# Per-head sums of squares by small fp32 matmuls with the squares as stationary operand, in an encoder block on one core

## The chip, the cores and the metric

The kernel runs on one core of a Trainium2 chip. The metric is the device time of one execution, in microseconds. Three runs of the kernel before gave 759.06, 760.45 and 761.18 us; the median is 760.45 us. One more execution was taken with the hardware profiler, and all times of single instructions come from it.

## The reference

One encoder layer on a sequence of 512 tokens of width 1024, all in fp32. What matters here is the attention group: the queries and the keys of eight heads are made from two small latents, and each head's 96 query numbers and 96 key numbers are normalised by their own root mean square (the key's 32 rotary numbers are shared by all heads).

```python
h = _rmsnorm(x, norm_mix)
proj = h @ w_in
c_q, c_kv, k_pe, u_h = ...                       # 768, 256, 32 and 3 * 512 wide
q  = (_rmsnorm(c_q, q_norm) @ w_uq).reshape(B, S, 8, 96)
kv = (_rmsnorm(c_kv, kv_norm) @ w_ukv).reshape(B, S, 8, 128)
k_nope, v = kv[..., :64], kv[..., 64:]
k = concatenate([k_nope, broadcast(k_pe)], -1)
q = _rmsnorm(q, qk_norm_q); k = _rmsnorm(k, qk_norm_k)
...                                              # rotary part, softmax(q k^T / sqrt(96)) v
u_h = _dwconv3(u_h); x0, x1, vh = split(u_h)     # Hyena: filters by a small sine network
y_hyena = x0 * _bidir_long_conv(x1 * vh, h_fwd, h_bwd, hyena_bias)
x = x + concatenate([_rmsnorm(y_attn), _rmsnorm(y_hyena)]) @ w_out
...                                              # gated MLP with a convolution, then an embedding term
```

## The kernel before, in words

All activations lie with the channel on the partitions and the 512 tokens along the free axis. A product of a weight with activations is done in three fp32r matmuls of 128x512: both operands are split into a high part (fp32r) and the rest, a low part, and high by high, high by low and low by high are summed in PSUM (`prod3`, `mms`, L176). The split of an activation is one ScalarE copy and one VectorE subtraction (`split`, L131 and L132, with a gain L134 and L135). Four PSUM banks named mm and four named ax are handed round.

Weights come in the order of the list `stream`. `wload` loads 128x1024 (or 128x768) by SyncE's queue, makes the high part on ScalarE (L142), and the low part in two ways: the first `cut` columns on VectorE (L143); the other columns by a negated copy on ScalarE (L145) to which a transfer on GpSimd's queue adds the weight from HBM once more (L146). There are three buffers of the high and of the low part, so the ScalarE instruction that makes the high part of a weight waits until TensorE has finished the product that used the weight three places earlier.

The order on TensorE is the order of the program text, with side work put in by a small planner: `advance(cost)` moves a clock while products are issued, and generators that are due on that clock issue their next piece between two groups of matmuls. The other engines' orders come from a scheduler with priorities (`pri`); each engine works its list strictly in that order. The stages up to the attention are:

- Input projection: 21 weights, 24 matmuls each. Two of them give the key/value latent, the third the rotary key. Beside it run two generators: `latent_kv`, which squares the two latent tiles (L519, L522), adds them into the tile accy (L523), after `D_LR` clock units makes the sum over the partitions by one fp32 matmul with a tile of ones (L220, in `rms_bcast`), and then the inverse root and the split (L205 to L216, L528, L134, L135); and `filter_task`, the sine network of the Hyena filter (three matmuls L370, each of which waits for ScalarE's sine L377 of the layer before), then the filter's transforms. `D_FT` is its start. Its last transform feeds a chain of VectorE products (L589 to L610) with eight results that ScalarE and VectorE split (L131, L132).
- UK: four products of 6 matmuls give the keys. Each is squared by `square` (L655, L131, L132) and copied (L723).
- UQ: six products of 18 matmuls give the queries, squared in the same way and copied (L773, L776). Into these the planner puts `key_task`, which sums the key squares of each head, makes 1/rms, and scales the keys; `query_scale` (turning of a row L231, four small fp32 matmuls L677); and `headsum_task`, which sums the query squares.
- The sums: `headsum` has 8 columns of 0 and 1 (`sel`) as stationary operand and the high and the low part of the squares as moving operand, two matmuls of 128x512, into 8 rows of one PSUM bank. After the last one, `rows` copies 8x512 out of PSUM on ScalarE (L667), and `turn_rows` turns it by four small transposes on TensorE (L231), so that tokens lie on the partitions; `rms_cols` does Ln, variance, Exp and one correction step on tiles of 128x32 (L205, L206, L210, L214 to L216). For the keys the result `ks` is turned back (L699), split (L701, L702) and spread over the partitions by matmuls L706.
- Then the values, the inverse transforms, and the attention (scores, softmax, transposes L942, weighing).

After the attention follow the output projection, the MLP and the embedding, which the change leaves alone.

## Time and profile before

| | before |
|---|---|
| median of 3 runs | 760.45 us |
| the profiled execution | 758.43 us |
| its span from first to last instruction | 756.6 us |
| TensorE busy | 722.1 us, 95% of the span |
| VectorE busy | 504.8 us, 67% |
| ScalarE busy | 372.2 us, 49% |
| mean granted TensorE clock | 0.991 |

1.83 us of the profiled execution lie outside the span. In a row of the timeline the first number is the start, the second the length, then engine, line, operation, output and inputs by name, and in brackets the idle time just before the row with the instruction that ended it. A row with "x6" is six instructions run together. The modelled length of a matmul overlaps the next one, so that the cost of a matmul is read from start to start.

### The profile page before, as it was taken

Reading aid. Unit: us, or ns where it says so; the run is one execution under the profiler, and the core shown is the slowest. Engines: PE = TensorE matmul, PEld = TensorE weight load, DVE = VectorE, ACT = ScalarE, POOL = GpSimd, SP = SyncE. Lnnn points to the kernel's source line nnn. Section 1 sums busy time; section 2 is a strip of 40 time slices with the busy share of each in tenths; the row PEclk is TensorE's granted clock in tenths of the full one; section 3 lists DMA queues with packets and bytes.
Section 4 is the critical chain, followed back from the end, with each engine's and each line's share of the span. In section 5 each row is a group of like instructions: output and inputs, shape, how many; then the busy total and the mean of one; then the engine's idle time right before and its main releaser. Section 6 shows DMA issues by size and latency. Waiting matters only on the chain.

```text
span 756.6 us, 9036 instructions
## 1 busy us (share of the span) xinstructions
PE 722.1 (95%) x3256; PEld 583.0 (77%) x3256; DVE 504.8 (67%) x780; ACT 372.2 (49%) x574; POOL 151.8 (20%) x150
## 2 busy tenths in 40 slices
PE   5989999996997899999999999999999999999997
PEld 4757888874675777787888888888888888888886
DVE  6479997989779987885766566666665332233382
ACT  7445455367658896463534443544353222126340
POOL 2101100111126662130422222222122000005000
PEclk9989999999899999999999999999999999999999
DMA  8844753444536210533232323232323233333331
GB/s 277 244 129 117 191 158 84 108 97 93 126 92 170 75 21 23 126 99 110 83 113 84 105 91 112 83 98 98 99 96 86 88 106 104 97 89 128 111 112 56
DMA packets 30110, 82.83 MB, mean 109 GB/s; under 512 B 3913, under 2 KB 5257, under 8 KB 30066
## 3 DMA queue, kind: packets, MB, share of 16 engines
q1 hardware_dynamic: 24418, 71.62, 31.1%
q0 software_dynamic: 5392, 10.25, 7.0%
q8 instruction: 25, 0.41, 0.2%
q10 hardware_dynamic: 256, 0.39, 0.2%
q14 instruction: 19, 0.16, 0.1%
HBM read 77.00 MB, written 2.10 MB: 105 GB/s over the span
## 4 chain that ended last, share of the span: by engine, by line
PE 54%; DVE 0%; ACT 0%; DVEq 0%; issue 0%
PE mm L176 37%; PE ax L176 17%; PE ax L220 0%; DVE t L1128 0%; ACT t L1127 0%; DVEq L1295 0%; DVE t L1129 0%
## 5 line engine op out<-in xcount | busy, mean ns | idle before, releaser
L176 PE MATMUL mm<-a,wh 128*128 128x512 f32 (+1 forms) x912 | 283.2, 392 | 8.2 <-ACT wh L273 6.5
L176 PEld LDWEIGHTS mm<-a,wh 128*128 128x128 f32 x912 | 171.0, 190 | 49.7 <-ACT wh L273 6.5
L143 DVE TENSOR_TENSOR wl<-wr,wh 128x1024 fp32r<-128x1024 f32 (+3 forms) x113 | 124.3, 1101 | 115.5 <-ACT wh L142 113.6
L142 ACT ACTIVATE wh<-wr 128x1024 fp32r<-128x1024 f32 (+1 forms) x113 | 116.5, 1031 | 162.3 <-PE mm L176 127.4
L176 PE MATMUL mm<-a,wl 128*128 128x512 f32 (+1 forms) x456 | 176.8, 388 | 0.0
L176 PE MATMUL ax<-a,wh 128*128 128x512 f32 x400 | 123.2, 389 | 0.0
L176 PEld LDWEIGHTS mm<-a,wl 128*128 128x128 f32 x456 | 86.2, 189 | 17.4 <-DVE wl L274 0.2
L176 PEld LDWEIGHTS ax<-a,wh 128*128 128x128 f32 x400 | 75.1, 188 | 15.5
L176 PE MATMUL ax<-a,wl 128*128 128x512 f32 x200 | 77.8, 389 | 0.0
L176 PE MATMUL mm<-g,wh 128*128 128x512 f32 x232 | 73.9, 401 | 1.7 <-ACT t L647 1.7
L1064 POOL TENSOR_TENSOR f<-f 128x512 f32<-128x512 f32 x22 | 28.7, 1304 | 169.2 <-DVE f L543 149.5
L176 PE MATMUL mm<-h,wh 128*128 128x512 f32 x192 | 59.0, 389 | 0.0
L176 PEld LDWEIGHTS mm<-g,wh 128*128 128x128 f32 x232 | 44.2, 192 | 12.9 <-ACT t L647 2.1
L176 PE MATMUL mm<-g,wl 128*128 128x512 f32 x116 | 46.0, 396 | 0.0
L176 PEld LDWEIGHTS ax<-a,wl 128*128 128x128 f32 x200 | 37.5, 188 | 7.9
L176 PEld LDWEIGHTS mm<-h,wh 128*128 128x128 f32 x192 | 36.0, 188 | 7.5
L1060 DVE TENSOR_TENSOR f<-mm,R 128x512 f32<-128x512 f32 x22 | 15.2, 691 | 33.7 <-PE mm L176 33.7
L176 PE MATMUL mm<-h,wl 128*128 128x512 f32 x96 | 37.3, 389 | 0.0
L536 ACT ACTIVATE f<-f,par 128x512 f32<-128x512 f32 x44 | 35.5, 808 | 1.0 <-DVE f L1060 1.0
L1063 ACT ACTIVATE f<-f 128x512 f32<-128x512 f32 x22 | 13.9, 632 | 44.5 <-DVE f L543 44.5
L146 POOL DMA_DIRECT2D wl<-in_w_in_dram x16 | 13.9, 868 | 106.0 <-ACT wl L145 53.0
L543 DVE SCALAR_TENSOR_TENSOR f<-f,par 128x511 f32<-128x511 f32 x44 | 33.8, 771 | 1.4
(312 smaller groups left out, 1015.9 us busy)
## 6 DMA issues: line engine op xcount, KB each, us to landing
wr<-in_w_up_dram SPq DMA_DIRECT2D x44, 512.0 KB, 3.5
wr<-in_w_in_dram SPq DMA_DIRECT2D x19, 512.0 KB, 3.9
wr<-in_w_down_dram SPq DMA_DIRECT2D x16, 512.0 KB, 3.5
x<-in_xT_dram SPq DMA_DIRECT2D x16, 256.0 KB, 4.3
wl<-in_w_in_dram POOLq DMA_DIRECT2D x16, 256.0 KB, 5.3
wr<-in_w_out_dram SPq DMA_DIRECT2D x8, 512.0 KB, 4.2
wr<-in_w_gate_dram SPq DMA_DIRECT2D x8, 512.0 KB, 3.5
wr<-in_w_down_dram SPq DMA_DIRECT2D x8, 384.0 KB, 3.0
```

Of the source, the lines that this page charges most:

```text
L142: S.activation(hi[:, :n], raw[:, :n], AF.Copy)
L143: V.tensor_tensor(lo[:, :cut], raw[:, :cut], f32(hi[:, :cut]), op=ALU.subtract)
L146: G.dma_start(lo[:, cut:n], src[:, cut:n], accum_op=ALU.add)
L176: last = PE.matmul(out, l, r, start=start and i == 0, stop=stop and i == n - 1)
L536: S.activation(c, z, AF.Identity, scale=pcol(w, 3 * m + 1), bias=pcol(b, m))
L543: V.scalar_tensor_tensor(c[:, 0 : T - 1], z[:, 1:T], pcol(w, 3 * m + 2), c[:, 0 : T - 1], op0=ALU.mult, op1=ALU.add)
L1060: V.tensor_tensor(z, ps_up.pop(m), R2, op=ALU.mult)
L1063: S.activation(cc[0], cc[0], AF.Silu)
L1064: G.tensor_tensor(cc[1], cc[0], cc[1], op=ALU.mult)
```

## The change

- `square` is one ScalarE instruction into a tile of its own; the split into high and low (one ScalarE copy, one VectorE subtraction) is gone, and with it the shared tile accy in between. There are ten such tiles, four for the keys and six for the queries.
- `headsum` issues four fp32 matmuls in place of two fp32r ones. 128 tokens of the squares are the stationary operand (128x128), 8 columns of `sel` the moving one; the result has tokens on the partitions and 8 columns. `rows` and the `turn_rows` of the keys' and queries' sums are gone. The keys' shared rotary square (`pesq`) goes the same way, in four small matmuls in place of one of 8x512.
- `key_task` spaces its sums by 0.9 in place of 0.5 clock units, and no longer waits `D_RC` before `rms_cols`.
- `sel` is fp32, loaded by SyncE's queue in place of GpSimd's.
- The first `cut` columns of a weight's low part, on VectorE, are 256 in place of 512 for the input projection from the sixth weight on and for the two UK/UV weights, and 256 in place of 384 for UQ. The other 768 or 512 columns take the way over ScalarE and the transfer.
- `D_LR` goes from 7 to 10 and `D_FT` from 8.5 to 11.5.

```diff
-D_LR = 7.0
+D_LR = 10.0
...
-D_FT = 8.5
+D_FT = 11.5
...
-    stream = [(w_in[m], 1024, 1024 if m < 5 else 512) for m in range(21)]
-    stream += [(w_ukn, 1024, 512)] + [(w_uq[m], 768, 384) for m in UQ] + [(w_ukv, 1024, 512)]
+    stream = [(w_in[m], 1024, 1024 if m < 5 else 256) for m in range(21)]
+    stream += [(w_ukn, 1024, 256)] + [(w_uq[m], 768, 256) for m in UQ] + [(w_ukv, 1024, 256)]
...
-    sel = const.tile([P, 56], F32R, tag="sel", name="sel")
+    sel = const.tile([P, 56], F32, tag="sel", name="sel")
...
+    SP.dma_start(sel, c_sel)
...
-        G.dma_start(sel, c_sel)
...
     def square(src):
         with pri("sq"):
-            S.activation(accy, src, AF.Square)
-            h, l = tmp(F32R), tmp(F32R)
-            split(h, l, accy)
-        return h, l
-
-    def headsum(ps, j, sq, start=False, stop=False):
-        w = sel[:, j * 8 : (j + 1) * 8]
-        mms(ps[0:8, :], [(w, sq[0]), (w, sq[1])], start=start, stop=stop)
-
-    def rows(ps):
-        r = tmp()[0:8, :]
-        with pri("rows"):
-            S.activation(r, ps[0:8, :], AF.Copy)
-        return r
+            sq = tmp()
+            S.activation(sq, src, AF.Square)
+        return sq
+
+
+    def headsum(ps, sq, w, start=False, stop=False):
+        for t in range(4):
+            PE.matmul(
+                ps[:, t * 8 : (t + 1) * 8], sq[:, t * P : (t + 1) * P], w,
+                start=start and t == 0, stop=stop and t == 3,
+            )
...
     def key_task(sqs):
         for j in range(4):
-            headsum(ssk, j, sqs[j], start=j == 0, stop=False)
-            yield 0.5
-        PE.matmul(ssk[0:8, :], ones[0:32, 0:8], pesq[0:32, :], start=False, stop=True)
-        k = rows(ssk)
-        yield D_RC
+            headsum(ssk, sqs[j], sel_of(j), start=j == 0, stop=False)
+            yield 0.9
+        headsum(ssk, pesq[0:32, :], ones[0:32, 0:8], stop=True)
         r = col("ks")
-        rms_cols(r, turn_rows(k), 96)
+        rms_cols(r, ssk[:, 0:32], 96)
         yield D_KC
...
     def headsum_task(j, sq):
-        headsum(ssq_ps, j, sq, not summed, len(summed) == 5)
+        headsum(ssq_ps, sq, sel_of(j), not summed, len(summed) == 5)
         summed.append(j)
-        if len(summed) == 6:
-            ssq_rows.append(rows(ssq_ps))
         yield None
...
-        rms_cols(v, turn_rows(ssq_rows[0]), 96, qs)
+        rms_cols(v, ssq_ps[:, 0:32], 96, qs)
```

In the changed kernel's own numbering `square` is L656, `headsum` L662, the turning of `ks` L696, its split L698 and L699, the copies of keys and queries L720, L768 and L771.

The planner and the scheduler put the instructions in another order at three places that matter.

**TensorE, fifth input weight.** mm_396 is the product of the fifth input weight and mm_480 or mm_440 that of the sixth; L220 is the latent's sum over the partitions, L370 the first layer of the sine network. Before, both stand behind 18 of the fifth product's 24 matmuls:

```order
L176 MATMUL mm_396<-a_152,wh_284 128x512
L176 MATMUL mm_396<-a_151,wl_285 128x512
L220 MATMUL ax_416<-accy_183,ones_81 128x512
L370 MATMUL ax_446<-x_191,x_190 128x512
L176 MATMUL mm_396<-a_155,wh_284 128x512
L176 MATMUL mm_396<-a_156,wh_284 128x512
```

Now L220 stands behind 6 matmuls of the sixth product, and L370 behind 6 more:

```order
L176 MATMUL mm_440<-a_129,wl_348 128x512
L220 MATMUL ax_448<-accy_183,ones_81 128x512
L176 MATMUL mm_440<-a_133,wh_347 128x512
L176 MATMUL mm_440<-a_134,wh_347 128x512
L176 MATMUL mm_440<-a_133,wl_348 128x512
L176 MATMUL mm_440<-a_139,wh_347 128x512
L176 MATMUL mm_440<-a_140,wh_347 128x512
L176 MATMUL mm_440<-a_139,wl_348 128x512
L370 MATMUL ax_484<-x_191,x_190 128x512
```

So 12 matmuls more come ahead of L220, and 18 more ahead of L370 when L220 is left out of the count.

**TensorE, fourth query product.** mm_1711 before and mm_1709 now are the fourth of the six query products. Before, the turning of the keys' row sums (t_1682 is ScalarE's copy of them) stands behind its first six matmuls:

```order
L176 MATMUL mm_1711<-g_1217,wh_1596 128x512
L176 MATMUL mm_1711<-g_1218,wh_1596 128x512
L176 MATMUL mm_1711<-g_1217,wl_1597 128x512
L231 MATMUL ax_1719<-ident_80,t_1682 128x8 x4
L176 MATMUL mm_1711<-g_1257,wh_1596 128x512
```

Now the turning of the finished key scales ks stands at the same place; before, that one (L699) came at the end of this product:

```order
L176 MATMUL mm_1709<-g_1201,wh_1581 128x512
L176 MATMUL mm_1709<-g_1202,wh_1581 128x512
L176 MATMUL mm_1709<-g_1201,wl_1582 128x512
L696 MATMUL ax_1716<-ident_80,ks_1675 8x128 x4
L176 MATMUL mm_1709<-g_1257,wh_1581 128x512
```

The instruction of this place is another one, and what it needs is further down the keys' chain.

**ScalarE, the same time.** These rows stand behind the one that makes the sixth query weight's high part (L142 of wh_1705 before, of wh_1703 now), which waits for the third query product. In the names a is the high part of a transform's result, g a query copy, col and ks the small tiles of `rms_cols`. Before, the copy L667 is the twelfth row behind it:

```order
L131 ACTIVATE a_1531<-t_1529 128x512
L145 ACTIVATE wl_1706<-wr_1703 128x384
L131 ACTIVATE a_1537<-t_1535 128x512
L131 ACTIVATE a_1543<-t_1541 128x512
L131 ACTIVATE t_1588<-accy_183 128x512
L131 ACTIVATE a_1549<-t_1547 128x512
L131 ACTIVATE a_1555<-t_1553 128x512
L655 ACTIVATE accy_183<-mm_1602 128x512
L773 ACTIVATE g_1656<-mm_1602,par_79 128x512
L131 ACTIVATE t_1652<-accy_183 128x512
L746 DMA qr_1874<-g_1656 64x512
L667 ACTIVATE t_1682<-ax_1440 8x512
```

Now the keys' variance (L206, the last small step of ScalarE for ks) is the thirteenth row behind it; the rows start at the second:

```order
L131 ACTIVATE a_1531<-t_1529 128x512
L656 ACTIVATE t_1575<-mm_1556 128x512
L768 ACTIVATE g_1577<-mm_1556,par_79 128x512
L131 ACTIVATE a_1537<-t_1535 128x512
L656 ACTIVATE t_1642<-mm_1587 128x512
L131 ACTIVATE a_1543<-t_1541 128x512
L145 ACTIVATE wl_1704<-wr_1701 128x512
L205 ACTIVATE qs_1423<-col_1621,eps_83 128x32
L206 ACTIVATE col_1620<-col_1621,eps_83 128x32
L210 ACTIVATE qs_1423<-qs_1423 128x32
L768 ACTIVATE g_1644<-mm_1587,par_79 128x512
L206 ACTIVATE col_1676<-ax_1432,eps_83 128x32
```

In both kernels nine instructions of 128x512 stand between; the last row is another one.

More of the change, by code (lines that the diff above doesn't have):

```diff
@@ L654, in square, with sel_of @@
         with pri("sq"):
-            S.activation(accy, src, AF.Square)
-            h, l = tmp(F32R), tmp(F32R)
-            split(h, l, accy)
-        return h, l
-    def headsum(ps, j, sq, start=False, stop=False):
-        w = sel[:, j * 8 : (j + 1) * 8]
-        mms(ps[0:8, :], [(w, sq[0]), (w, sq[1])], start=start, stop=stop)
-    def rows(ps):
-        r = tmp()[0:8, :]
-        with pri("rows"):
-            S.activation(r, ps[0:8, :], AF.Copy)
-        return r
+            sq = tmp()
[7 more added lines that the diff above has]
+            )
+    def sel_of(j):
+        return sel[:, j * 8 : (j + 1) * 8]
     qs = col("qs")
@@ L675, in query_scale @@
         ps = ax_ps()
-        for t in range(4):
-            PE.matmul(ps[:, t * 8 : (t + 1) * 8], accx[:, t * P : (t + 1) * P], ones[:, 0:8], start=True, stop=True)
+        headsum(ps, accx, ones[:, 0:8], True, True)
         rms_cols(qs, ps[:, 0:32], 768, r1)
@@ L753, in tile_encoder_block @@
     ssq_ps = ax_ps()
-    summed, ssq_rows = [], []
+    summed = []
     def headsum_task(j, sq):
-        headsum(ssq_ps, j, sq, not summed, len(summed) == 5)
+        headsum(ssq_ps, sq, sel_of(j), not summed, len(summed) == 5)
         summed.append(j)
-        if len(summed) == 6:
-            ssq_rows.append(rows(ssq_ps))
         yield None
```

## The prediction

> **What bounds the kernel now.** I read the page first, then the table of TensorE's waits, then the clock by stage, and only then single rows. From the page, the span, the busy times and the chain that ended last:
>
> ```profile
> span 756.6 us, 9036 instructions
> PE 722.1 (95%) x3256; PEld 583.0 (77%) x3256; DVE 504.8 (67%) x780; ACT 372.2 (49%) x574; POOL 151.8 (20%) x150
> PE 54%; DVE 0%; ACT 0%; DVEq 0%; issue 0%
> ```
>
> TensorE is the bound, and the chain is TensorE alone over the later 54% of the span, where nothing is changed. So an edit counts by what it does, ahead of that, to TensorE's own time and to its waits. The waits near the change (in total, how often, the longest):
>
> ```profile
> PE ax L231 <- ACT t L667: 6.7, 2, 6.0
> PE ax L220 <- DVE accy L523: 2.9, 1, 2.9
> PE mm L176 <- ACT t L647: 1.7, 1, 1.7
> PE ax L370 <- ACT x L377: 0.7, 1, 0.7
> ```
>
> The copy of the row sums costs 6.7 us, 6.0 of them at the keys; the latent's sum waits 2.9 us. In the windows view the third number from the end is the granted clock:
>
> ```profile
> 40.00:60.00 20.00, 19.23 (x61) 12.60 (x62) 16.00 (x27) 11.27 (x16) 1.73 (x2) 0.83 0.44 114
> 180.00:200.00 20.00, 14.01 (x55) 10.71 (x53) 15.18 (x35) 14.78 (x30) 1.73 (x2) 0.83 0.34 83
> 240.00:260.00 20.00, 19.10 (x113) 15.38 (x112) 19.06 (x45) 18.15 (x40) 13.22 (x14) 1.00 0.25 67
> ```
>
> The clock falls to 0.83 in the windows that hold these two waits, so each is paid twice: once idle, once in slow matmuls behind it.
>
> **The latent's sum, 12 matmuls later.** TensorE's timeline from this wait on:
>
> ```profile
> 40.10 1.97 PE L220 MATMUL ax<-accy,ones 128*128 128x512 f32 x2 [2.91 <-DVE accy L523]
> 42.01 2.07 PE L370 MATMUL ax<-x 33*128 33x512 f32 x2
> 44.01 1.22 PE L176 MATMUL mm<-a,wh 128*128 128x512 f32 x2
> 46.74 0.78 PE L176 MATMUL mm<-a,wh 128*128 128x512 f32 x2
> ...
> 55.91 1.12 PE L370 MATMUL ax<-x 64*128 64x512 f32 x2 [0.67 <-ACT x L377]
> 56.96 0.73 PE L176 MATMUL mm<-a,wh 128*128 128x512 f32 x2
> ```
>
> And two pieces of the chain at full clock, an L220 and a product of 24 matmuls:
>
> ```profile
> 347.26 0.86 PE ax L220 x2
> 353.58 5.44 PE ax L176 x24
> ```
>
> One 128x512 matmul at full clock is 5.44 / 24 = 0.227 us. Behind the wait L220 takes 42.01 - 40.10 = 1.91 where 0.86 is normal, the sine network's L370 44.01 - 42.01 = 2.00 where the later one takes 56.96 - 55.91 = 1.05, and six matmuls 46.74 - 44.01 = 2.73 where 6 x 0.227 = 1.36 is normal. The low clock costs 1.05 + 0.95 + 1.37 = 3.4 us.
>
> TensorE came to L220 at 40.10 - 2.91 = 37.19; with 12 x 0.227 = 2.7 us of products ahead it comes at 39.9. What it waits for comes a little later too, since a low part now has 768 columns on ScalarE in place of 512 ahead of the latent's squares:
>
> ```profile
> 39.36 0.69 DVE L523 TENSOR_TENSOR accy<-accy,t 128x512 f32<-128x512 f32 x1
> ```
> ```profile
> 35.62 0.61 ACT L145 ACTIVATE wl<-wr 128x512 fp32r<-128x512 f32 x1
> ```
> ```profile
> L142 ACT ACTIVATE wh<-wr 128x768 fp32r<-128x768 f32 x6 | 5.1, 847 | 8.4 <-issue 5.7 <-PE mm L176 2.8
> ```
>
> A copy of 768 columns is 0.85 us by the nearest form, 0.24 more, and two such lie on the way: the sum ends at 39.36 + 0.69 + 0.48 = 40.5. A wait of about 0.6 us is left, too short to lower the clock (0.67 us at 55.91 did not). Gain: 2.3 us of wait and 3.4 of clock. Ends: no wait at all, 0.6 better; 1.1 left, 0.5 worse.
>
> The network's second and third layer stay at about the same distance from the first, but the sines' VectorE steps now stand behind the latent's. The wait of 0.67 may go or grow and the third layer may wait as much. Between -0.7 and +1.6 I take +0.9, since VectorE is busy for 16.0 of the 20 us there.
>
> **The filter, one half product later.** Its last transform comes 18 matmuls (4.1 us) later among the input products, and VectorE's chain of products starts from it. Where that chain ended before:
>
> ```profile
> 162.31 0.74 DVE L135 SCALAR_TENSOR_TENSOR g<-mm,par,g 128x512 fp32r<-128x512 f32 x1
> ```
> ```profile
> 163.97 0.73 PE L176 MATMUL mm<-g,wh 128*128 128x512 f32 x2 [1.65 <-ACT t L647]
> ```
> ```profile
> 164.46 1.28 ACT L244 ACT_TABLE_LOAD   x1
> ```
>
> TensorE waited 1.65 us for a PSUM bank that ScalarE's copy L647 frees, which follows VectorE's L135. In the new order VectorE's last L135 stands ahead of the second half of the products (six instructions of L523's size), so that it ends at about the old time; but ScalarE then has the key squares and the table load ahead of the first key copy. Followed row by row I get a wait of 1.1 at the fourth UK product (L647) and 1.5 at the first UQ product (first key copy, behind the table load): 2.6 in place of 1.65, +1.0. Without the six products behind L135 it would be +4.1; with VectorE ahead by what the shorter split saves it, -0.5.
>
> **The sums themselves.** Query-scale has the new form already, four fp32 matmuls with 128 tokens stationary; behind it stands an old pair:
>
> ```profile
> 173.69 1.06 PE L677 MATMUL ax<-ones,accx 128*128 128x8 f32 x8
> 174.60 0.62 PE L176 MATMUL ax<-t,sel 128*8 128x512 f32 x2
> 175.06 0.63 PE L176 MATMUL mm<-g,wh 128*128 128x512 f32 x2
> ```
> ```profile
> L677 PEld LDWEIGHTS ax<-ones,accx x8: 186/192/192, 173.7 to 174.5; 128*128 128x128 f32 x8
> ```
>
> From start to start, the new form is 174.60 - 173.69 = 0.91 us and the old 0.46: ten sums cost 10 x 0.45 = +4.5 us, all on TensorE's path. The eight records for four matmuls have eight weight loads; they, and not the 8 columns, fill the time. The shared rotary square was one fp32 matmul of 512 columns (0.86 as L220) and becomes a group of 0.91: +0.05.
>
> The Trainium skill, "TensorE: Matmul & The Clock Gate", section "LDWEIGHTS (loading the stationary operand)", speaks against this form: loading takes about the number of columns over 1.2 GHz, however few rows are used. By it eight loads of 128 columns are an estimated 0.85 us, the ten sums +3.9, and the whole sum 0.6 lower; the trace's 0.91 is a little dearer, and I go by the trace.
>
> Two sets of four transposes L231 leave; one took 188.87 - 188.35 = 0.52 us below at the low clock, and I take 0.35 each: -0.7.
>
> **The keys' wait.** The copy it waits for, and what follows:
>
> ```profile
> 180.80 0.85 ACT L142 ACTIVATE wh<-wr 128x768 fp32r<-128x768 f32 x1 [0.68 <-PE mm L176]
> ...
> 187.71 0.59 ACT L667 ACTIVATE t<-ax 8x512 f32<-8x512 f32 x1
> ```
> ```profile
> 188.35 0.59 PE L231 MATMUL ax<-ident,t 8*128 8x8 f32 x4 [5.99 <-ACT t L667]
> 188.87 1.22 PE L176 MATMUL mm<-g,wh 128*128 128x512 f32 x2
> ...
> 194.02 0.60 PE L699 MATMUL ax<-ident,ks 128*8 128x128 f32 x4
> ```
>
> The copy did not wait for its sums (its row has no bracket). It stood in ScalarE's list behind L142, which at 180.80 had to wait for TensorE's third query product to free its buffer, and behind eleven more: it came 187.71 + 0.59 - 180.80 = 7.5 us after L142, while TensorE needs only six matmuls (1.4 us) from the same event to this place. The change takes away the copy, but puts at this very place of TensorE's order the turning of ks, and ks needs ScalarE's L206, which stands thirteenth behind the same L142, with nine instructions of 128x512 between, and then three small steps on VectorE. So by about 7.4 to 7.9 us after L142 ks is there: the wait of 6.0 does not go, it changes its name. I take 0; ends -0.5 and +0.6. The slow matmuls behind it (194.02 - 188.87 = 5.15 for twelve, where 2.72 is normal: 2.4 us) stay too.
>
> At the queries two short waits go:
>
> ```profile
> 212.25 0.41 PE L231 MATMUL ax<-ident,t 8*128 8x8 f32 x4 [0.68 <-ACT t L667]
> 216.34 1.43 PE L176 MATMUL ax<-ks,qs 96*128 96x512 f32 x5 [0.22 <-DVE ks L749]
> ```
>
> The first with its copy, the second since 3 us of new sums stand ahead: -0.9.
>
> **The stream and the removed splits.** Ten VectorE and ten ScalarE instructions leave, and VectorE's part of a low part shrinks; TensorE waits for none of these rows. The transfer grows from 256 to 384 KB, for UQ from 192 to 256, and its columns are needed after 6 matmuls in place of 12:
>
> ```profile
> wl<-in_w_in_dram POOLq DMA_DIRECT2D x16, 256.0 KB, 5.3
> wl<-in_w_uq_dram POOLq DMA_DIRECT2D x6, 192.0 KB, 4.1
> ```
> ```profile
> 61.66 0.86 POOL L146 DMA_DIRECT2D wl<-in_w_in_dram  x1 [6.59 <-DVE wl L143]
> ```
> ```profile
> 73.80 0.39 PE L176 MATMUL mm<-a,wl 128*128 128x512 f32 x1
> ```
>
> The two sizes differ by 1.2 us per 64 KB, so 384 KB land after an estimated 7.7 us. The transfer issued at 61.66 (one of the tightest) serves the product whose third low matmul starts at 73.80: 12.1 us, less 0.24 for the wider copy, so 4 us are spare. Cost 0; beyond that cover each product would wait by what is lacking.
>
> **Sum.** -2.3 - 3.4 + 0.9 + 1.0 + 4.5 + 0.05 - 0.7 + 0 - 0.9 = -0.9 us (rounded). Against the profiled execution's 758.43 that is 757.5. The median of the runs is 2.0 above that execution, so on its scale 760.45 - 0.9 = 759.5. A measurement here can tell about 0.3% (2.3 us) from no change.
>
> **Rivals.**
> 1. The keys' wait falls below what lowers the clock. For it: both engines have less to do (ten instructions each), and if the a splits between L142 and L206 run early, ks comes sooner. Against it: the order is strict and L142 cannot start before the third query product ends. Price: 3.1 less waiting and the 2.4 of clock, -0.9 - 5.5 = -6.4: 754.1. Chance 0.25.
> 2. The filter's delay lands in full in front of UK: VectorE's chain is 4.1 us later and TensorE waits 1.65 + 4.1 = 5.8, long enough for the low clock. It decides once VectorE's last L135 ends more than about 1.5 us after its old time relative to TensorE. Against it: the six products moved behind L135. Price: -0.9 - 1.0 + 4.1 + 2.4 = +4.6: 765.0. Chance 0.15.
> 3. The clock gate catches another gap. At the attention's start there is a wait as long as the latent's:
>
> ```profile
> 239.81 0.93 PE L176 MATMUL ax<-ks,qs 96*128 96x512 f32 x3 [2.94 <-DVE ptl L132]
> ```
>
> It did not lower the clock (1.00 from 240 to 260), while 2.91 at 40.10 did. Everything ahead shifts by a microsecond or two, so it could now: +2.4 to +3.4, together 761.9 to 762.9. Chance 0.10. The Trainium skill, "TensorE: Matmul & The Clock Gate", section "Part 1: The HAM clock gate", says that the clock halves after an idle window of about 3.4 us that runs freely; by that rule, gaps just under it go either way, and the trace agrees with its 2.91 and 2.94.
>
> **How the numbers follow.** My forecast has 0.50, with its own range of 757.2 to 761.8 from the ends above. Faster by over 0.3% (below 758.2): all of the first rival and a fifth of the forecast, 0.36. Slower by over 0.3% (above 762.7): the second, half of the third and a little of the forecast, 0.22. Within: 0.42. The range, 753.5 to 764.0, takes in the first rival's centre and stops short of the second's: about 0.2 is left out.
>
> **What would show it.** Right: no slow clock behind L220, which waits well under a microsecond; L662 groups 0.9 us apart; L696 waiting 5 to 6.6 us with a clock of about 0.83 in its window; two waits of 1 to 2 us between UK and UQ; no wait on a transfer of wl. Wrong: a short or missing wait at L696, a UK wait over 3 us, or a second low clock elsewhere.

## The result, and the profile after

The changed kernel took 769.43 us in the median of four runs (766.7 to 771.24), the kernel before 760.75 us in four (759.06 to 761.18). The ratio is 1.0115, with a 95% interval of 1.008 to 1.015: the change is slower by more than the 0.3% that can be told here, and the time lies outside the range of 753.5 to 764.0. The profiled execution took 766.70 us with a span of 764.9; the mean granted TensorE clock was 0.983 in it, 0.991 before. From here on "before" and "after" are the two kernels, and line numbers are those of the kernel that is spoken of.

The page of after, its span, its busy times and the clock by slices of 19 us:

```profile
span 764.9 us, 9129 instructions
PE 729.9 (95%) x3314; PEld 595.2 (78%) x3314; DVE 492.3 (64%) x770; ACT 369.5 (48%) x562; POOL 151.0 (20%) x149
PEclk9999999998889999999999999999999999999999
```

The span grew by 8.3 us, TensorE's busy time by 7.8. Three slices in a row (172 to 229 us, where the new sums stand) are below nine tenths. TensorE's waits in after, those that answer to the list of before:

```profile
PE ax L696 <- DVE ks L216: 5.4, 1, 5.4
PE ax L176 <- DVE g L132: 4.3, 1, 4.3
PE mm L176 <- ACT x L720: 1.3, 1, 1.3
PE ax L220 <- DVE accy L523: 1.2, 1, 1.2
PE mm L176 <- ACT t L647: 0.9, 1, 0.9
```

The latent's wait fell from 2.9 to 1.2 and the sine network's 0.7 is gone. The keys' wait has the new name L696 and is about as long as the old 6.0. The filter's two waits are 0.9 and 1.3. The second line is new: 4.3 us that no step of the prediction contains. TensorE's timeline of after, at the places that were forecast and at the new ones:

```profile
41.07 1.13 PE L220 MATMUL ax<-accy,ones 128*128 128x512 f32 x2 [1.17 <-DVE accy L523]
...
94.60 1.03 PE L553 MATMUL ax<-ident,uu 128*128 128x128 f32 x8
...
100.83 2.93 PE L176 MATMUL ax<-g,dft 128*128 128x512 f32 x6 [4.32 <-DVE g L132]
...
165.28 0.74 PE L176 MATMUL mm<-g,wh 128*128 128x512 f32 x2 [1.31 <-ACT x L720]
...
173.15 0.95 PE L662 MATMUL ax<-sel,t 128*128 128x8 f32 x8
...
174.37 1.06 PE L662 MATMUL ax<-ones,accx 128*128 128x8 f32 x8
175.29 1.09 PE L176 MATMUL mm<-g,wh 128*128 128x512 f32 x2
...
192.35 1.01 PE L696 MATMUL ax<-ident,ks 128*8 128x128 f32 x4 [5.36 <-DVE ks L216]
193.02 1.20 PE L176 MATMUL mm<-g,wh 128*128 128x512 f32 x2
...
197.18 0.61 PE L176 MATMUL mm<-g,wh 128*128 128x512 f32 x2
...
213.70 4.39 PE L662 MATMUL ax<-sel,t 128*128 128x8 f32 x32
217.95 5.43 PE L176 MATMUL mm<-a,dft 128*128 128x512 f32 x12
223.21 1.52 PE L176 MATMUL ax<-ks,qs 96*128 96x512 f32 x6
```

Before, the same places in TensorE's timeline read:

```profile
101.46 1.03 PE L553 MATMUL ax<-ident,uu 128*128 128x128 f32 x8
...
212.59 3.02 PE L176 MATMUL mm<-a,dft 128*128 128x512 f32 x12
215.62 0.50 PE L176 MATMUL ax<-ks,qs 96*128 96x512 f32 x1
```

Two things are to be seen. The transposes L553 start at 94.60 in place of 101.46: before, six matmuls of the filter's first transform (1.4 us) stood ahead of them, so 5.5 us had been won by there. Of that the transform, now right behind the transposes, loses 4.32 at once. And the twelve dft products behind the four last query sums take 223.21 - 217.95 = 5.26 us, where before they took 215.62 - 212.59 = 3.03: they run slowly, without a wait ahead of them. The windows view of after says why; the third number from the end is the granted clock:

```profile
100.00:104.00 4.00, 3.17 (x8) 2.55 (x9) 2.57 (x5) 0.46 (x2) 0.00 (x0) 0.57 0.01 3
176.00:180.00 4.00, 4.00 (x17) 3.40 (x17) 0.86 (x2) 2.25 (x4) 0.07 (x1) 0.65 0.01 2
212.00:216.00 4.00, 4.00 (x32) 3.73 (x31) 0.11 (x1) 1.33 (x3) 0.00 (x0) 1.00 1.05 220
216.00:220.00 4.00, 4.00 (x17) 3.61 (x18) 1.08 (x5) 1.64 (x5) 0.00 (x0) 0.55 0.41 122
```

At 100 the clock fell behind a wait. At 176 and 216 TensorE was busy for the whole 4.00 us, and in the stretch ahead of 216 too; just ahead of the low clock stood small matmuls (173.15 to 175.29 and 213.70 to 217.95). Summed in windows of 2 us from 20 to 270 us, (1 - clock) x time is 6.8 us before and 12.0 after. It comes in portions of 1.7 us, that is 3.4 us at half clock: before two at the latent's wait and two at the keys'; after one behind the filter's new wait, one behind query-scale, two at the keys', two behind the last four query sums, and one at the attention's gap (246 to 252). Seven in place of four, all in the one profiled execution of each kernel.

Start of the same work in both traces, in us:

| place | before | after | difference |
|---|---|---|---|
| transposes L553, the filter's 6 matmuls allowed for | 100.1 | 94.60 | -5.5 |
| first query product | 163.97 | 165.28 | +1.3 |
| turning of the keys (L231 before, L696 after) | 188.35 | 192.35 | +4.0 |
| first scores | 215.62 | 223.21 | +7.6 |
| the chain's 24 products in the MLP | 341.79 | 350.15 | +8.4 |

### The profile page after: what moved, and what is told of

It reads as the page before. It is cut to its first block, busy times and chain, and to the rows that moved or that the text cites. A ratio compares the mean times of both kernels' runs of the same rounds, so it can differ in the third digit from the quotient of the medians.

```text
span 764.9 us, 9129 instructions
## 1 busy us (share of the span) xinstructions
PE 729.9 (95%) x3314; PEld 595.2 (78%) x3314; DVE 492.3 (64%) x770; ACT 369.5 (48%) x562; POOL 151.0 (20%) x149
## 4 chain that ended last, share of the span: by engine, by line
PE 54%; DVE 0%; ACT 0%; DVEq 0%; issue 0%
PE mm L176 36%; PE ax L176 17%; PE ax L220 0%; DVE t L1123 0%; ACT t L1122 0%; DVEq L1290 0%; DVE t L1124 0%
## 5 line engine op out<-in xcount | busy, mean ns | idle before, releaser
L142 ACT ACTIVATE wh<-wr 128x1024 fp32r<-128x1024 f32 (+1 forms) x113 | 116.6, 1031 | 170.5 <-PE mm L176 130.6
L143 DVE TENSOR_TENSOR wl<-wr,wh 128x1024 fp32r<-128x1024 f32 (+3 forms) x113 | 118.6, 1051 | 116.8 <-ACT wh L142 115.1
```

The source lines that it names most:

```text
L142: S.activation(hi[:, :n], raw[:, :n], AF.Copy)
L143: V.tensor_tensor(lo[:, :cut], raw[:, :cut], f32(hi[:, :cut]), op=ALU.subtract)
```

## The experiments

There were two theories of the missing time, which may both hold for a part. The collision: the later start of the filter puts its first transform where four PSUM banks are held by work that waits on VectorE, 4.3 us and a portion of low clock. The clock: 8-column matmuls in a row count as idle for the clock, though TensorE always has an instruction. Rivals were the plain number of matmuls, the smaller VectorE part of the stream, and the keys' wait.

All results, in the order of the four sets; each set has its own runs of before, and the ratio is to those:

| kernel | median us | before | ratio, 95% interval |
|---|---|---|---|
| b_delay | 762.85 | 760.89 | 1.002, 1.000 to 1.004 |
| b_sums | 764.61 | 760.89 | 1.007, 1.003 to 1.011 |
| b_stream | 761.61 | 760.89 | 1.001, 1.000 to 1.002 |
| a_wide | 756.88 | 760.89 | 0.995, 0.993 to 0.996 |
| a_w16 | 765.59 | 760.99 | 1.008, 1.006 to 1.011 |
| a_w64 | 765.06 | 760.99 | 1.005, 1.002 to 1.008 |
| a_kc | 763.60 | 760.99 | 1.006, 1.003 to 1.009 |
| a_ft | 766.21 | 760.99 | 1.008, 1.005 to 1.011 |
| m8x16 | 799.68 | 760.36 | 1.051, 1.047 to 1.055 |
| m64x16 | 788.35 | 760.36 | 1.036, 1.032 to 1.040 |
| m8x8 | 773.71 | 760.36 | 1.017, 1.013 to 1.021 |
| c_w128_ft10_5 | 758.70 | 760.36 | 0.997, 0.996 to 0.999 |
| a_oldstream | 769.09 | 760.52 | 1.012, 1.010 to 1.014 |
| c_w128_oldstream | 755.36 | 760.52 | 0.995, 0.993 to 0.997 |
| b_delay_rc | 764.69 | 760.52 | 1.008, 1.005 to 1.011 |

The three m kernels have two runs each, the others four to ten, before 13 to 22 in each set. What is said to be under or over after (769.43, four runs) goes across sets, in which the median of before moves by 0.6 us.

### One part at a time: b_delay, b_sums, b_stream

Three kernels, each before with one part of the change. Three dots stand for code that is not printed.

b_delay, the two delays alone:

```diff
-D_LR = 7.0
+D_LR = 10.0
-D_FT = 8.5
+D_FT = 11.5
```

> The kernel before with the two delays alone (latent 7 to 10, filter 8.5 to 11.5). Theory A (the later filter collides with the forward transform: its first transform needs a PSUM bank that VectorE frees only behind a product that waits for the decay table): the wait of about 4 us at the filter's first transform and a low clock of 1 to 2 us behind it are there, the latent's wait is about 1 us with no low clock behind it; together the time is that of before, -1 to +2 us. Theory C (the wait needs the larger transfers of the new stream): no wait over 1 us at that place, the time is 4 to 6 us under before.

Measured: 762.85, 2.0 us over before. Its timeline has the new wait at the same place, half as long:

```profile
99.81 2.91 PE L176 MATMUL ax<-g,dft 128*128 128x512 f32 x6 [2.05 <-DVE g L132]
```

The waits list of b_delay has two more lines that had been shorter before:

```profile
PE ax L231 <- ACT t L667: 10.5, 2, 9.8
PE ax L370 <- ACT x L377: 1.9, 1, 1.9
```

So the delays make the collision without any other part of the change. The latent's wait and its low clock went, as forecast; the keys' wait, which the prediction left at 6.0, rose to 9.8, and with the waits of 2.0 and 1.9 it ate the gain.

b_sums, everything else of the change: the squares, the sums and their spacing, with the delays and the stream as before:

```diff
-        mms(ps[0:8, :], [(w, sq[0]), (w, sq[1])], start=start, stop=stop)
+        for t in range(4):
+            PE.matmul(ps[:, t * 8 : (t + 1) * 8], sq[:, t * P : (t + 1) * P], w, ...)
```

> The kernel before with the new sums alone (one square, small fp32 matmuls, no row copies). Theory B (a run of small matmuls of 8 columns counts as idle for the clock): the clock falls behind the four query sums that stand in a row and perhaps near query-scale, though TensorE is never without an instruction there; 5 to 9 us slower than before. Rival (only the matmuls' own time counts): 2 to 3.5 us slower, the clock low only behind the latent's sum and the keys' wait as before.

Measured: 764.61, 3.7 us over before, from 761.82 to 770.99. The median lies between the two forecasts, so it is the trace that decides. The keys' wait is 2.6 us, less than half of before's, and the kernel is slower all the same. A window of b_sums, among its sums and query products:

```profile
184.00:188.00 4.00, 4.00 (x15) 3.52 (x14) 0.98 (x2) 0.00 (x0) 0.00 (x0) 0.50 0.67 174
```

TensorE has no idle moment in it (4.00 busy) and runs at half clock. The profiled execution lost 17.1 us of clock, ten portions, four of them behind sums without a wait (182 to 190 and 218 to 228), and took 769.76, one of the three slow ones of seven. The runs follow their clock: 761.82 us at 0.984, 770.99 at 0.974.

b_stream, the smaller VectorE part alone:

```diff
-    stream = [(w_in[m], 1024, 1024 if m < 5 else 512) for m in range(21)]
-    stream += [(w_ukn, 1024, 512)] + [(w_uq[m], 768, 384) for m in UQ] + [(w_ukv, 1024, 512)]
+    stream = [(w_in[m], 1024, 1024 if m < 5 else 256) for m in range(21)]
+    stream += [(w_ukn, 1024, 256)] + [(w_uq[m], 768, 256) for m in UQ] + [(w_ukv, 1024, 256)]
```

> The kernel before with the new split of the weights alone (256 columns on VectorE). Theories A and B: within 1.5 us of before, no wait of TensorE on a transfer. Theory C (larger transfers crowd the queues and delay the decay tables): 3 us or more slower, with VectorE waiting for a decay table and TensorE behind it.

Measured: 761.61, a ratio whose interval includes 1. By itself the stream costs nothing that can be told.

### The moving columns: a_wide, a_w16, a_w64

In after every sum moves 8 columns. These kernels move N = 128, 16 or 64 columns through the same number of matmuls with the same stationary loads; of every N results only the first 8 are read, the others are useless sums. So the arithmetic that counts and the output stay.

```diff
-                ps[:, t * 8 : (t + 1) * 8], sq[:, t * P : (t + 1) * P], w,
+                ps[:, t * N : (t + 1) * N], sq[:, t * P : (t + 1) * P], w,
...
-        return sel[:, j * 8 : (j + 1) * 8]
+        return sel[:, j * 8 : j * 8 + N]
...
-        rms_cols(r, ssk[:, 0:32], 96)
+        rms_cols(r, eight(ssk), 96)
```

`eight` takes the first 8 of each N columns. The tile of 0 and 1 has 176 columns in them, the last 120 of them 0.

> The changed kernel with 128 moving columns in place of 8 in every small sum (the other 120 results are not used; the 8 that are used are the same numbers). Theory B: a group takes 0.9 to 1.2 us, and the clock stays at 1.00 behind query-scale and behind the last four query sums, so it is 3 to 6 us faster than the changed kernel (about 763 to 766). Rival (fp32 matmuls or chance of the clock's phase): the clock falls at the same two places, and it is as slow as the changed kernel or up to 3 us slower.

Measured: 756.88, 12.5 us under after and 4.0 under before. TensorE's timeline of a_wide at the last sums and at the keys:

```profile
186.24 0.60 PE L700 MATMUL ax<-ident,ks 128*8 128x128 f32 x4 [0.39 <-DVE ks L216]
...
205.95 3.73 PE L663 MATMUL ax<-sel,t 128*128 128x128 f32 x32
209.44 2.98 PE L176 MATMUL mm<-a,dft 128*128 128x512 f32 x12
```

And windows of a_wide, behind query-scale and behind the last sums:

```profile
176.00:180.00 4.00, 4.00 (x26) 3.53 (x25) 3.58 (x6) 2.58 (x5) 0.40 (x1) 1.00 0.02 6
212.00:216.00 4.00, 4.00 (x19) 3.26 (x18) 2.94 (x7) 1.41 (x3) 0.00 (x0) 1.00 0.01 2
```

Sixteen times the columns and the sums are not longer: the four last take 209.44 - 205.95 = 3.49 us, against 217.95 - 213.70 = 4.25 with 8 columns, part of which ran at the low clock. At whole clock a group takes 0.80 with 128 columns and 0.81 with 8. The twelve products behind the last four run at full speed. The clock stays at 1.00 at both places. But the test was not clean. In a_wide ScalarE's step L206 stands ahead of a copy L142 that it stood behind in after, so the keys' wait, 5.36 in after, is 0.39. It loses four portions of clock in place of seven: none at the sums and the keys, where after has five, but two behind the filter's wait and two at the attention's gap, where after has one each. So the 12.5 us mix the columns with the keys' order. The next two kernels keep the keys' order of after.

> The changed kernel with 16 moving columns in place of 8 in the small sums; the order at the keys' wait is that of the changed kernel. Theory B (the clock goes by how much of the time the array streams columns): 16 columns are still far too few, the clock falls behind query-scale and behind the last four query sums as in the changed kernel, time within 2 us of it (767 to 771). Rival (any longer small matmul will do): the clock stays at 1.00 at both places, 4 to 6 us faster.

Measured: 765.59. The keys' wait is 5.2 in it as in after, and in its profiled execution the clock is low only behind waits (98 to 107, 190 to 196, 242 to 250), not behind the sums. The theory had 16 columns still too few, and this execution contradicts that. The time, 3.8 us under after, falls between the two forecasts, and the runs, from 764.25 at 0.988 to 768.8 at 0.983, leave room for executions in which the clock does fall behind the sums.

> The changed kernel with 64 moving columns; the order at the keys' wait (the variance thirteenth behind the copy of a weight) is still that of the changed kernel, so that wait of about 5.4 us stays. Theory B: a group still takes about 0.9 us, the clock stays at 1.00 behind query-scale and behind the last four query sums, and the time is 4 to 7 us under the changed kernel (762 to 765). Rival (what the kernel with 128 columns gained came from its other order on ScalarE): the clock falls as in the changed kernel and the time is within 2 us of it.

Measured: 765.06. The clock is at 1.00 at all sums, and the profile's 6.8 us of lost clock, four portions, lie behind the filter's wait (one), behind the keys' (one) and at 260 to 268 (two). Two waits are new, in the waits list of a_w64:

```profile
PE mm L176 <- DVE a L135: 2.9, 4, 1.9
PE mm L176 <- ACT a L134: 2.0, 1, 2.0
```

So with the keys' wait still there (4.3 us), wide sums bring 4.4 us of the 12.5. The other 8.1 lie elsewhere: a_wide has 3.9 us less of the keys' wait and none of the low clock behind it, and it lacks the 3.9 us of these two new waits.

### The keys' wait and the filter's place: a_kc, a_ft

a_kc is after with more clock units ahead of the turning of the keys:

```diff
-D_KC = 2.5
+D_KC = 8.0
```

> The changed kernel with the turning of the key scales about 27 product matmuls later on TensorE (D_KC 8 in place of 2.5). The keys' wait is a matter of order: it falls from 5.4 us to under 1, the low clock in it goes too (1.6 us), and nothing else waits instead: 5 to 8 us faster than the changed kernel (762 to 764). Rival: the attention's start waits for the scaled keys instead, and the gain is under 2 us.

Measured: 763.60, 5.8 us under after. No line for `ks` is left among its waits. The time is as expected, but something else does wait instead: the two new waits of a_w64 are here too (1.9 and 2.0 us). And the sums now stand closer together. TensorE's timeline of a_kc:

```profile
208.04 5.12 PE L662 MATMUL ax<-sel,t 128*128 128x8 f32 x24
```

Three groups stand in a row and take 4.97 us to the next row's start, 1.7 each, where 0.91 was the price in before; they run at half clock from their start. With the keys' wait gone the low clock at the sums stays (206 to 217, three portions), and the time of its runs goes with the clock: 760.51 us at 0.986, 769.39 at 0.976.

a_ft is after with the filter's old start:

```diff
-D_FT = 11.5
+D_FT = 8.5
```

> The changed kernel with the filter's old start (D_FT 8.5; the latent's later sum stays). Theory A (the filter's first transform stands right behind the forward transform's four transposes and waits for their PSUM banks): with the old start it stands 24 matmuls ahead of them, the wait of 4.3 us and the 1.7 us of low clock behind it go, 4 to 7 us faster (763 to 766). Rival (the decay table's late transfer is the cause wherever the transform stands): a wait of 2 us or more for it stays.

Measured: 766.21, only 3.2 us under after, which the spread of four runs (763.63 to 769.49) hardly sets apart. The waits list of a_ft:

```profile
PE mm L176 <- ACT t L647: 2.7, 1, 2.7
PE ax L176 <- DVE g L414: 2.6, 1, 2.6
PE ax L370 <- ACT x L377: 2.0, 1, 2.0
```

The collision's 4.3 us are gone, but three other waits, at the sine network, at the filter's first product and at the key products, sum to 7.3. The keys' wait is gone as well (no line for L696 is left), so that TensorE waits less in all than in after. What eats the gain is the clock: this execution lost 15.3 us of it where after lost 12.0, and four portions stand in a row from 182 to 196, with no wait ahead of them or in them. Two windows of a_ft:

```profile
182.00:186.00 4.00, 4.00 (x15) 3.54 (x14) 2.06 (x4) 0.63 (x2) 0.27 (x1) 0.52 0.64 111
186.00:190.00 4.00, 4.00 (x14) 3.03 (x14) 0.00 (x0) 0.15 (x1) 0.00 (x0) 0.50 0.23 90
```

Ahead of them stand 2.1 us of small matmuls (179.30 to 181.44): four small transposes, query-scale's group and a key sum. The collision belongs to the new start, yet its price of 6 us is not the gain of undoing it.

### The disputed cost by itself: m8x16, m64x16, m8x8

Before, with useless work added in the MLP, where the chain is TensorE alone: eight runs of G fp32 matmuls with N moving columns each, into a free PSUM bank that nobody reads. N and G are 8 and 16, 64 and 16, 8 and 8.

```diff
+            if s == 1 and f in (4, 6, 8, 10, 12, 14, 16, 18):
+                ps = ax_ps()
+                for t in range(G):
+                    PE.matmul(ps[:, (t % 4) * N : (t % 4 + 1) * N], (ones, ident)[t % 2], ones[:, 0:N], start=True, stop=True)
```

> The kernel before with eight runs of 16 useless fp32 matmuls of 8 columns put into the MLP, where TensorE works without a wait (their results are not used). Own time by the 0.228 us of the changed kernel's sums: 8 x 16 x 0.228 = 29 us. Theory B: each run (3.6 us) counts as idle, and 3.4 to 6.8 us of products behind it go at half clock, 1.7 to 3.4 us each: 43 to 56 us slower than before in all. Rival (only own time counts): 29 us slower, the clock in the MLP stays at 1.00.

> The same eight runs with 64 columns in place of 8. Theory B: the same own time, 29 to 32 us, and no low clock: 29 to 32 us slower than before. Rival (fp32 matmuls or the breaks in the stream lower the clock whatever their width): as the kernel with 8 columns, 43 us or more.

> Eight runs of 8 useless matmuls of 8 columns (1.8 us each) in the MLP. Own time 8 x 8 x 0.228 = 14.6 us. Theory B with a window of about 3.4 us: half a window of dense products remains, so the clock falls at none or few of them, 14 to 20 us slower than before. If any short stretch of small matmuls lowers the clock: 28 us or more.

Measured against before: +39.3, +28.0 and +13.4 us. Windows of m8x16 behind one of its runs:

```profile
420.00:424.00 4.00, 4.00 (x30) 3.78 (x30) 2.83 (x4) 1.04 (x2) 0.90 (x1) 0.92 0.38 88
424.00:428.00 4.00, 4.00 (x13) 3.16 (x12) 0.00 (x0) 0.63 (x1) 1.66 (x2) 0.66 0.11 45
```

And the window of m64x16 behind the same run:

```profile
420.00:428.00 8.00, 8.00 (x49) 7.06 (x49) 2.61 (x3) 1.44 (x3) 2.59 (x2) 1.00 0.20 67
```

With 64 columns the 128 added matmuls cost 28.0 / 128 = 0.219 us each and the clock stays whole through the MLP. With 8 columns the same number costs 11.3 us more. TensorE is busy for all of these windows, and the clock falls behind six of the eight runs (the windows that start at 420, 448, 476, 528, 556 and 580), by (1 - 0.92) x 4 + (1 - 0.66) x 4 = 1.7 us at this one and the same at the others: 6 x 1.7 = 10.2 of the 11.3. That is less than the 43 to 56 us that the theory expected, since two runs cost no clock and the others one portion each. With eight matmuls a run, 1.8 us, the clock does not fall in the MLP at all, and 13.4 is about half of 28.0. This is the clean test that a_wide was not: same place, same number, same stationary loads, and nothing waits.

### Can the collision be moved away: c_w128_ft10_5, a_oldstream, c_w128_oldstream, b_delay_rc

c_w128_ft10_5 is a_wide with the filter's start between the old and the new (`D_FT = 10.5`).

> The changed kernel with 128 moving columns and D_FT 10.5, which puts the filter's first transform six product matmuls ahead of the forward transform's four transposes. Theory A: the wait of 4.3 us for their PSUM banks is gone or under 1.5, and so is the low clock behind it: 3 to 6 us under the kernel with 128 columns alone (751 to 754). Rival (the transform then waits for its own decay product, which waits for the same late table): a wait of 3 us or more at the same place, same time (756 to 758).

Measured: 758.70, no better than a_wide's 756.88, so neither forecast came. The wait went to the sine network (L371, 1.25 and 1.70 us) and to the filter's product (L415, 2.7), and the clock fell for one portion behind each of the three.

a_oldstream is after, c_w128_oldstream is a_wide, each with the two lines of `stream` as before, in which VectorE has the larger part of a low part:

```diff
-    stream = [(w_in[m], 1024, 1024 if m < 5 else 256) for m in range(21)]
-    stream += [(w_ukn, 1024, 256)] + [(w_uq[m], 768, 256) for m in UQ] + [(w_ukv, 1024, 256)]
+    stream = [(w_in[m], 1024, 1024 if m < 5 else 512) for m in range(21)]
+    stream += [(w_ukn, 1024, 512)] + [(w_uq[m], 768, 384) for m in UQ] + [(w_ukv, 1024, 512)]
```

> The changed kernel with the old split of the weights (512 and 384 columns on VectorE). If the delays alone make the wait at the filter's first transform: it is there, and the wait there and at the sine network's second layer together come to about what the kernel before with the delays alone showed (2.0 + 1.9 us); time within 2 us of the changed kernel. If the larger transfers make it: the wait falls below 1 us and the time by 4 us or more.

Measured: 769.09, the same as after. Its waits:

```profile
PE ax L176 <- DVE g L132: 2.0, 1, 2.0
PE ax L370 <- ACT x L377: 1.9, 1, 1.9
```

Waits of 2.0 and 1.9 stand where after has 4.3 at one place. The stream shifts the wait between the two places and doesn't make it.

> The same with 128 moving columns in the small sums: the clock behind query-scale and behind the last four sums stays at 1.00, so 5 to 12 us under the one with 8 columns. If the larger transfers cost nothing, within 2 us of the changed kernel with 128 columns (755 to 759), unless ScalarE's order puts the keys' wait back (then 5 us more).

Measured: 755.36 us in ten runs (754.76 to 760.46), 5.2 us under before (ratio 0.993 to 0.997) and 14 under after. With a_wide (0.993 to 0.996) it is the fastest here; the two can't be told apart. Its waits at these places:

```profile
PE ax L176 <- DVE g L132: 2.4, 2, 2.1
PE ax L371 <- ACT x L378: 1.9, 1, 1.9
PE ax L700 <- DVE ks L216: 1.4, 1, 1.4
```

One portion of clock (1.7 us) is lost in its profiled execution, behind the attention's gap, in place of four before and seven after. In this execution no new wait and no sum lowered the clock. The runs reach up to 760.46 at 0.989, so in others more is lost. With 8 columns the same stream gained nothing.

b_delay_rc is b_delay with the pause `D_RC` ahead of the keys' rows raised to 6.5, to see whether b_delay's wait of 9.8 us could be filled.

> The kernel before with the two delays and with the keys' row turning 18 product matmuls later (D_RC 6.5): whether the keys' wait can be had away without the new sums. In ScalarE's order the row copy stands 15 instructions (about 8 us) behind the copy that waits for the third query product, TensorE has 24 matmuls (5.4 us) in that time: the wait falls from 9.8 us in the kernel with the delays alone to 2 to 4, 5 to 9 us under it (754 to 758). Rival: the wait moves along with the matmul as the keys' did in the changed kernel, 6 us or more stay, same time (761 to 764).

Measured: 764.69, a little slower than even the rival had it, though L231's wait fell from 10.5 to 0.7. The waits list, from the slowest of the five runs (770.01), has two others in its place:

```profile
PE ax L706 <- DVE t L702: 5.2, 1, 5.2
PE mm L176 <- DVE wl L143: 5.1, 1, 5.1
```

The next step of the same chain waits instead, and a product waits for the low part of its weight from VectorE. So a later place in TensorE's order alone did not help; that ScalarE's and VectorE's lists are what is late there is argued from these two lines, not tried.

## Why the prediction was wrong

**The bound, and the latent's sum: right.** The forecast was a wait of 0.6 us without low clock behind it; it is 1.17, and the clock is 1.00 from 40 to 60 us. By L553 5.5 us are won. The term of +0.9 for the sine network's later layers was not paid: after has no wait there.

**The filter: the end was right, the start was not looked at.** The step followed the last transform and got two waits of 1.1 and 1.5; they are 0.9 and 1.3. It priced the delay at the end of VectorE's chain only. The delay also moves the first transform, from 24 matmuls ahead of the transposes L553 to right behind them. This is the first step that failed, a term that the sum lacks: 4.3 us of wait and a portion of low clock, about 6 together. VectorE's timeline of after shows what it waits for:

```profile
94.09 1.30 DVE L439 TENSOR_TENSOR t<-ax,t 128x512 f32<-128x512 f32 x2 [3.46 <-DMA t<-in_c_dec_dram]
...
100.09 2.48 DVE L132 TENSOR_TENSOR g<-ax,g 128x512 fp32r<-128x512 f32 x4
```

The transfer's issue on SyncE's queue in after, and the same VectorE row in before:

```profile
87.64 0.90 SPq L432 DMA_DIRECT2D t<-in_c_dec_dram  x2
```
```profile
92.16 1.31 DVE L439 TENSOR_TENSOR t<-ax,t 128x512 f32<-128x512 f32 x2 [0.63 <-DMA t<-in_c_dec_dram]
```

The transposes fill the four banks named ax, which come free by the splits L132. These stand in VectorE's strict list behind L439, which waits 3.46 us for the decay table (0.63 before), issued at 87.64 and there at 94. The first splits start at 100.09, TensorE goes on at 100.83. So a late table holds four PSUM banks by way of an instruction that has nothing to do with them. b_delay has this wait without the sums and the stream, a_ft lacks it without the filter's delay: that the later start makes it is shown. How much of it is the table's lateness was not tried by itself; VectorE's wait for the table and TensorE's behind it are 1.95 and 2.05 us in b_delay, 3.46 and 4.32 in after.

**The sums themselves: right as time, wrong as a whole; this is the second step that failed.** It said "ten sums cost 10 x 0.45 = +4.5 us". At whole clock the groups are 0.81 to 0.91 us from start to start in after, a little under the 0.91 assumed. But the step took a busy TensorE for a TensorE that keeps its clock. Two portions behind the last four sums and one behind query-scale are 5.1 us on top, and m8x16 against m64x16 shows the effect alone. Query-scale's one group of four stands in before too and did not lower the clock there; the step stretched that one row over ten groups.

The kernels taken together say the same. At the last four sums the profiled executions of all five kernels with 8 columns (after, b_sums, a_kc, a_ft, a_oldstream) lose one to three portions, those of the five with 16 columns or more none. Behind query-scale, where about 2.1 us of small matmuls stand together, four of the five with 8 columns lose one to four (a_kc does not), and again none of the wider ones.

The Trainium skill, "TensorE: Matmul & The Clock Gate", section "Part 1: The HAM clock gate", has the clock halved after an idle window of about 3.4 us and given back after a busy one. The portions agree: 1.7 us lost is 3.4 us at half clock, and all totals here (1.7, 6.8, 8.5, 10.2, 12.0, 13.7, 15.3, 17.1 us) are near whole numbers of them. What the runs add is that the clock also falls though a matmul was always under way, if these had 8 columns. And less than a whole window is enough: one that ran freely and had to be idle throughout would seldom fit into a run of 3.5 us, where six of eight lowered the clock, and never into 2.1 us. The prediction took the rule to leave gaps just under 3.4 us open; taken at its word it lets none of them count, while the waits of 2.91 us here, and of 1.25 and 1.70 in c_w128_ft10_5, did. The measurement decides, and the border is not known.

**The keys' wait: right.** 5.4 where 6.0 was forecast, under the new name, with the same two portions at it. The low clock began at about 189 already, while TensorE was empty, so that the twelve matmuls behind it took 197.18 - 193.02 = 4.16 us: 1.4 over the normal 2.72, where 2.4 was forecast. The first rival (this wait falls) came in a_wide, a_ft, c_w128_oldstream and, by half, b_sums, each with another order on ScalarE; it did not come in after.

**The stream: right.** No wait on a transfer, and b_stream costs nothing.

**The rivals.** The second (the filter's delay lands in full at the key products) did not come, though its price of +4.6 was near that of the collision, which stands 60 us earlier. The third came: the gap at the attention, as long as before, lowered the clock. TensorE's timeline of after:

```profile
246.77 1.33 PE L176 MATMUL ax<-ks,qs 96*128 96x512 f32 x3 [2.93 <-DVE ptl L132]
```

Its price is one portion, at most 1.7 us (0.8 by the table of starts) where 2.4 to 3.4 was forecast. So 2.94 and 2.93 us at the same place went either way.

**The sum.** Forecast 757.5 for the profiled execution, measured 766.7: 9.2 us are missing. Dearer came out the collision with its portion, 6.0, the sums' three portions, 5.1, the latent's longer wait, 0.6, and the attention's portion, of which no more than 0.8 was paid by the table (8.4 - 7.6): 12.5 together. Cheaper came out the sine network, 0.9, the filter's end, 0.4, the keys' wait, 0.6, the slow matmuls behind it, 1.0, and the ten groups, about 0.5 by the 0.86 of those at whole clock: 3.4 together. The difference is 9.1; that it comes so near is in part luck, for each term is read to about 0.2.

## What to carry to other kernels

When a producer is delayed, follow its first step as well as its last: what it now stands behind, which PSUM banks are held there, and what the engine that frees them is waiting for. A long row of matmuls with few moving columns is priced by its stationary loads and by what it does to the clock behind it; padding the moving side to 64 or 128 columns cost no time here and took the low clock away. A wait that is moved is usually found again one step on, so a pause is judged by the whole list of waits and the lost clock, not by the line that vanished.

## What the runs showed of the hardware

- 8-column fp32 matmuls in a row let the granted clock fall to half without TensorE being without work: behind six of eight runs of 3.5 us in m8x16, behind none of eight runs of 1.8 us in m8x8, and behind the 2.1 us at query-scale in after, b_sums, a_ft and a_oldstream, but not in a_kc. 64 columns kept the clock whole in a run of 3.5 us (m64x16).
- Waits much shorter than the 2.91 us at L220 can lower it too: 1.25 and 1.70 us at L371 in c_w128_ft10_5 and 1.84 at L370 in b_delay_rc did, for one or two portions, while 1.87 at L370 in b_delay and a_oldstream did not.
- Such a matmul with 128 stationary columns cost 0.219 us with 64 moving columns, and a group of four was no longer with 128 columns than with 8 (0.80 in a_wide, 0.81 in after, at whole clock). The Trainium skill, "TensorE: Matmul & The Clock Gate", section "LDWEIGHTS (loading the stationary operand)", puts a load at the number of columns over 1.2 GHz; for the two loads of each matmul that is an estimated 0.213 us, and the runs agree.
- Open: what decides whether a short wait or a short run of small matmuls lowers the clock, whether the border lies between 8 and 16 columns (one profiled execution of a_w16), why the late waits of a_w64 and a_kc at L134 and L135 (4.9 us in all) come, and what the wide sums would give without the delays, which wasn't tried.
